# First layer of a two-layer decoder on one core: attention probabilities turned by VectorE and DRAM transfers in place of TensorE

## The chip, the core and the metric

The kernel runs on one core of one Trainium2 chip. The metric is the device time of one execution in microseconds (us). TensorE (PE, and PEld for its weight loads), VectorE (DVE), ScalarE (ACT) and GpSimd (POOL) each work through a list of instructions in order; SP issues the transfers of the weights, POOL the transfers told of below.

## The reference, cut to what matters

A trunk of two layers, 256 tokens of width 2048, all float32. The first layer is forgetting attention with 32 heads of 64, the second sliding-window attention; only the first is touched.

```python
p = rmsnorm(x, norm_g[0]) @ fox_w_in        # q, k, v, gate, forget logits
c = cumsum(log_sigmoid(forget logits + b_f))            # per head
s = einsum('qd,kd->qk', q, k) / 8 + c[q] - c[k]         # causal: k <= q
y = softmax(s) @ v * silu(gate)
x = x + y @ fox_w_out
```

Queries are swept in blocks of 128. For one head the first block sees 128 keys and the second 256, so the probabilities of a head are three blocks of 128 queries by 128 keys. The product with v contracts over keys, so keys must lie on the partitions: each block has to be turned.

## The kernel before

**Weights.** Every weight matrix comes in pieces of 512 KB (`wraw`, four buffers). ACT casts a piece to its high half (L222), DVE subtracts to get the low half (L223), both into `w` (five buffers), and TensorE multiplies high and low halves (`acc`). `mm` and `transpose` keep TensorE in the order in which the program is written.

**Groups.** The heads of layer one are eight groups of four, a group two pairs of heads (j = 0, 1). A group's units are q, k and gate, of 16 slices of the contraction each; an odd group also computes v for itself and the next one. When k of a group is there, `attend` hangs the attention steps on a clock: `tick()` counts, one step per two matmuls (in v units two steps per three), and `after(n, fn)` runs fn n steps later. So the tables `FOX_DUE`, `FOX_ODD`, `FOX_FIRST` and `FOX_NEXT` say between which weight matmuls each piece of attention stands.

**A pair.** `early` fetches the row -c[k] to all partitions (`bc`, a POOL transfer, L649) and masks it (L125, POOL), 14 steps ahead. `s` forms the scores of the second query block into the one score buffer in PSUM (`ps_s`), DVE adds the bias (L430) and finds the maxima (L411). `s_first` does the same for the first query block (L442) some steps later, in the same buffer. Then ACT takes exponentials (L359) and DVE normalises `st` (L367, L370). `t`, once per head, has TensorE turn three blocks by matmuls against the identity (`pt`, L84), and ACT copies them to `pts` (L451).

**Values.** At `due[2]`, an even group multiplies `pts` of the previous odd group and of its own with v (`psy`, 16 matmuls a group); groups 0 and 7 do so alone. DVE multiplies by the gate (L534), ACT and DVE split the result into `ys`. The tile `pts` of even groups and that of odd groups have one buffer each; `bc` and `st` have two.

**Layer two** already turns its probabilities by a DVE transpose of 32x32 blocks (L497), multiplies per 32-row strip, and sends v through DRAM once (`vs_d`, L889, L896, L897). That part stays.

Of the kernel before, what the change touches and what calls it, by code (L numbers as in the profile page):

```python
# [19 lines left out]
KT = D // P  # L20
H = 32
HD = 64
KVH = 4
ROT = 16
EPS = 1e-6
# [34 lines left out]
def trunk(  # L60
# [22 lines left out]
    def transpose(out, in_, ident):  # L83
        tc.keep_in_program_order(nc.tensor.transpose(out, in_, ident))  # L84
# [235 lines left out]
    def each(row):  # L320

        return row.unsqueeze(1).to_broadcast([P, 2, S])
# [69 lines left out]
    class Pair:  # L392
# [54 lines left out]
        def t(self, hh, group):  # L447
            pt = ps_t.tile([P, 512], F32, tag="T", name="pt")
            for b in range(3):
                transpose(pt[:, b * P : (b + 1) * P], self.st[:, hh, b * P : (b + 1) * P], ident)  # L450
            nc.scalar.copy(group.new_pts(self.j, hh)[:, hh, self.j, :], pt[:, 0 : 3 * P])  # L451

        def later(self, group, s, t, second=SECOND, bias=BIAS, other=4):
            self.second = second
            after(s - bias, self.early)
            after(s, self.s)
            after(t, lambda: self.t(0, group))
            after(t + other, lambda: self.t(1, group))

    class JointPair(Pair):  # L460

# [31 lines left out]
            after(t, lambda: self.both_t(group))  # L493

        def both_t(self, group):
            turned = group.new_pts(self.j, 0)[:, group.u % 2 * 2 + self.j]
            nc.vector.transpose(  # L497
                turned.rearrange("p h k -> p (h k)"), self.st.rearrange("p h k -> p (h k)")
            )

    class Group:
# [1 line left out]

        pts_home = work, "pts"

        def new_pts(self, j, hh):

            if j == hh == 0:
                pool, tag = self.pts_home
                self.pts = pool.tile([P, 2, 2, 3 * P], F32, tag=tag, name="pts", bufs=1)  # L510
            return self.pts

        def attend(self, kt, due, together, same):
            self.kt = kt
            for j, steps in enumerate(due[0:2]):
                self.pair(j).later(self, *steps)
            if together:
                after(due[2], lambda: self.values(together, same))

        def values(self, together, same):  # L520

            psys = []
            for G in together:
                psy = ps_t.tile([P, 512], F32, tag="T", name="psy")
                psys.append(psy)
                for js in [slice(0, 2)] if same else [slice(j, j + 1) for j in range(2)]:
                    for hh in range(2):
                        o = psy[hh * HD : (hh + 1) * HD, :].rearrange("p (j n) -> p j n", j=2)[:, js, :]
                        p = G.pts[:, hh, js, :]
                        v = [G.v_of(js.start, b, hh) for b in range(2)]  # L530
                        mm(o, v[0], p[:, :, 0:S], start=True, stop=False)
                        mm(o[:, :, P:S], v[1], p[:, :, S : 3 * P], start=False, stop=True)
# [51 lines left out]
    class FoxGroup(Group):  # L584
# [3 lines left out]
            self.g = g  # L588

        def q(self, ps):  # L590
            t = fox.tile([P, 2, S], F32, tag="q", name="q", bufs=1)
            nc.vector.tensor_add(t, ps[:, :, 0:S], low_half(ps))
            nc.vector.tensor_mul(t, t, each(state["r08"][:, 0:S]))
            self.qT = stack_q(t)

        def k(self, ps):
            t = fox.tile([P, 2, S], F32, tag="k", name="k", bufs=1)
            nc.vector.tensor_add(t, ps[:, :, 0:S], low_half(ps))
            nc.vector.tensor_mul(t, t, each(r0()[:, 0:S]))  # L599

            kk = self.kT = fox.tile([P, 2, 2, 2, S], F32R, tag="kk", name="kk", bufs=KBUFS)
            for hh, (w, other) in enumerate(((TOP, BOTTOM), (BOTTOM, TOP))):
                nc.scalar.copy(kk[w, :, hh, 0, :], t[w])
                nc.scalar.copy(kk[other, :, hh, 0, :], t[w])
                high = kk[w, :, hh, 0, :].bitcast(F32)
                nc.vector.tensor_sub(kk[w, :, hh, 1, :], t[w], high)  # L606
                nc.vector.tensor_sub(kk[other, :, hh, 1, :], t[w], high)  # L607
            due = (FOX_FIRST, FOX_NEXT, FOX_DUE, FOX_ODD)[min(self.g, 2 + self.g % 2)] if self.g < 7 else FOX_DUE
# [5 lines left out]
            self.attend(2 * self.g, due, mates, False)  # L614

        def v_pair(self, other):

# [278 lines left out]
                nc.gpsimd.dma_start(out=most[rows], in_=blocks[:, 0:6])  # L896
                nc.gpsimd.dma_start(out=rest[rows], in_=blocks[:, 6:8])  # L897

    B, NB = 32, P // 32
    vs_d = dram.tile([S, 256], F32, name="vs_d")  # L900

    class SwaGroup(Group):
# [5 lines left out]
        def q(self, ps):  # L908
            with tc.high_priority(HP):
                t, u = rotate(ps)  # L910
                nc.vector.tensor_add(t, t, u)
                self.qT = stack_q(t)

            self.attend(2 * self.u, SWA_DUE if self.u < 7 else SWA_LAST, (self.other, self) if self.u % 2 else (), True)

        def pair(self, j):
            h0 = 4 * self.u + 2 * j
# [18 lines left out]
            pair.bias = smask.unsqueeze(1).to_broadcast([P, 2, 3 * P])  # L936
            return pair

        def new_pts(self, j, hh):
# [5 lines left out]
        def values(self, together, same):  # L945

            if self.u < 7:
                self.some(together, range(NB), ps_s.tile([P, 2, 512], F32, tag="S", name="psy_s"))
                return
            self.some(together, range(2))  # L950
            after(LAST_HALF, lambda: self.some(together, range(2, NB)))

        def some(self, together, mine, pair=None):
# [25 lines left out]
            for g, G in enumerate(together):  # L979
# [224 lines left out]
```

## Time and profile before

| | |
|---|---|
| three timed runs | 813.56, 814.32, 814.44 us, median 814.32 |
| profiled execution, its own time | 814.33 us |
| its span, first to last instruction | 812.6 us |
| TensorE busy, granted clock | 802.0 us, 0.997 |
| DVE, ACT, POOL busy | 635.2, 529.6, 68.1 us |
| moved by transfers | 151.84 MB, mean 187 GB/s |

Work on layer one's attention lies between about 64 and 420 us of the span. Idle time of an engine costs only where TensorE, or whatever else sets the end, waits for it. A group's row in the list of groups gives how many instructions, their busy time in total and the mean of one; matmuls are pipelined, so their busy times overlap, and what a matmul takes from the end is better read from the chain of waits, whose pieces add up to the span.

### The profile page before, as it was taken

To read this page: it belongs to the slowest core of one execution; us is meant where nothing else is said; L and a number is where in the kernel's file an instruction comes from. 1 tells how busy PE (TensorE), PEld (TensorE's weight loads), DVE (VectorE), ACT (ScalarE), POOL (GpSimd) and SP (SyncE) were. 2 spreads that over 40 slices of the span, in tenths; PEclk is the share of its full clock that TensorE was granted. 3 is DMA by queue.
4 is the path that set the end of the run, shared out by engine and by line. 5 is a ranking of instruction groups with operands and counts; after the bars stand their busy time and mean duration, and the time that the engine had idled before them with its cause. 6 is when DMAs were issued, how large, how long until landed. Compare 5 with 4: busy or idle time off the path is not lost.

```text
span 812.6 us, 13809 instructions
## 1 busy us (share of the span) xinstructions
PE 802.0 (99%) x5090; PEld 705.6 (87%) x5090; DVE 635.2 (78%) x1132; ACT 529.6 (65%) x979; POOL 68.1 (8%) x102
## 2 busy tenths in 40 slices
PE   8999999999999999999999999999999999999996
PEld 7988788888888888888888888888888888888885
DVE  6988876887678776788847778678999999987654
ACT  6876665674756666575746555577788777875652
POOL 1012120010000100010003110200000000001210
PEclk9999999999999999999999999999999999999998
DMA  8767565564565655565455655766446544565632
GB/s 271 260 222 237 184 200 185 176 221 160 197 203 171 210 181 194 183 209 167 156 183 168 219 180 196 195 182 201 137 157 206 181 162 152 157 191 197 195 124 104
DMA packets 47730, 151.84 MB, mean 187 GB/s; under 512 B 5696, under 2 KB 7648, under 8 KB 47664
## 3 DMA queue, kind: packets, MB, share of 16 engines
q1 hardware_dynamic: 44640, 141.84, 53.6%
q0 software_dynamic: 1872, 7.67, 3.2%
q10 hardware_dynamic: 1152, 1.47, 0.5%
q8 instruction: 40, 0.66, 0.3%
q14 instruction: 26, 0.21, 0.1%
HBM read 148.55 MB, written 2.41 MB: 186 GB/s over the span
## 4 chain that ended last, share of the span: by engine, by line
PE 97%; DVE 2%; DMA 1%; ACT 0%; issue 0%; DVEq 0%; SPq 0%
PE acc L81 90%; PE ps_s L81 3%; PE psy L81 2%; PE pt L84 1%; DMA wraw<-in_vf_dram 1%; DVE w L223 0%; PE psy_s L81 0%; DVE st L370 0%; DVE scaled L836 0%; DVE q L389 0%; DVE kk L607 0%; ACT st L359 0%; DVE kk L606 0%; PE ps_n L81 0%; DVE k L599 0%
## 5 line engine op out<-in xcount | busy, mean ns | idle before, releaser
L81 PE MATMUL acc<-xs,w 128*128 128x256 f32 (+1 forms) x2624 | 473.1, 338 | 0.0
L81 PEld LDWEIGHTS acc<-xs,w 128*128 128x128 f32 x2624 | 405.7, 190 | 53.3 <-issue 0.7
L223 DVE TENSOR_TENSOR w<-wraw,w 128x1024 fp32r<-128x1024 f32 (+4 forms) x277 | 322.3, 1177 | 102.7 <-ACT w L222 101.8
L222 ACT CAST w<-wraw 128x1024 fp32r<-128x1024 f32 (+4 forms) x277 | 274.1, 1009 | 154.4 <-PE acc L81 122.2
L81 PE MATMUL acc<-ys,w 128*128 128x256 f32 (+1 forms) x960 | 168.8, 337 | 0.0
L81 PEld LDWEIGHTS acc<-ys,w 128*128 128x128 f32 x960 | 147.4, 190 | 19.3 <-issue 0.5
L81 PE MATMUL acc<-w,xs 128*128 128x512 f32 (+2 forms) x512 | 111.0, 364 | 1.5 <-ACT w L222 1.5
L81 PEld LDWEIGHTS acc<-w,xs 128*128 128x128 f32 x512 | 86.8, 190 | 15.8 <-ACT w L222 1.8
L359 ACT ACTIVATE st<-st,mx 128x256 f32<-128x256 f32 (+1 forms) x128 | 56.5, 443 | 12.5 <-DVE mx L411 7.1
L317 ACT COPY half<-acc 128x512 f32<-128x512 f32 x56 | 32.7, 584 | 36.9 <-PE acc L81 36.5
L741 POOL TENSOR_TENSOR acc<-acc,sq 128x256 f32<-128x256 f32 x28 | 26.7, 955 | 82.5 <-ACT sq L735 81.4
L81 PE MATMUL ps_s<-kk,q 128*128 128x256 f32 (+1 forms) x160 | 30.9, 306 | 0.2 <-DVE kk L607 0.2
L81 PEld LDWEIGHTS ps_s<-kk,q 128*128 128x128 f32 x160 | 24.7, 190 | 3.3 <-ACT pts L451 0.6
L649 POOL DMA_DIRECT2D bc<-negc_d x16 | 8.8, 553 | 220.4 <-DVE st L442 159.2
L125 POOL TENSOR_SCALAR_AFFINE_SELECT bc<-bc 128x256 f32<-128x256 f32 x32 | 21.7, 699 | 62.2 <-DMA bc<-negc_d 62.2
L739 POOL COPY acc<-sq 128x256 f32<-128x256 f32 x2 | 1.3, 636 | 288.2 <-ACT sq L735 288.2
L378 ACT ACTIVATE st<-st,rl 128x128 f32<-128x128 f32 x64 | 23.9, 445 | 0.4 <-ACT gate_e L335 0.3
L359 ACT ACTIVATION_READ_ACCUMULATOR st<-st,mx 128x1 f32 x128 | 24.0, 188 | 0.0
L157 DVE SCALAR_TENSOR_TENSOR xs<-xT,g_sb,xs 128x256 fp32r<-128x256 f32 x32 | 20.4, 666 | 3.5 <-ACT xs L156 3.5
L451 ACT COPY pts<-pt 128x384 f32<-128x384 f32 x32 | 15.2, 476 | 8.7 <-PE pt L84 8.5
L156 ACT ACTIVATE xs<-xT,g_sb 128x256 fp32r<-128x256 f32 x32 | 15.5, 502 | 8.1 <-DVE xT L721 7.4
L411 DVE CUSTOM_DVE_ANT_0 st<-ps_s,st 128x256 f32<-128x256 f32 (+1 forms) x64 | 20.2, 352 | 0.4
(144 smaller groups left out, 579.4 us busy)
## 6 DMA issues: line engine op xcount, KB each, us to landing
wraw<-in_fox_in_dram SPq DMA_DIRECT2D x96, 512.0 KB, 4.2
wraw<-in_swa_in_dram SPq DMA_DIRECT2D x72, 512.0 KB, 4.4
wraw<-in_fox_out_dram SPq DMA_DIRECT2D x32, 512.0 KB, 4.5
wraw<-in_swa_out_dram SPq DMA_DIRECT2D x32, 512.0 KB, 4.5
wraw<-in_fox_in_dram SPq DMA_DIRECT2D x54, 256.0 KB, 4.1
bc<-negc_d POOLq DMA_DIRECT2D x16, 384.0 KB, 4.6
wraw<-in_vf_dram SPq DMA_DIRECT2D x4, 288.0 KB, 5.8
xT<-in_xt_dram SPq DMA_DIRECT2D x2, 512.0 KB, 8.2
```

What stands on the lines that cost most here:

```text
L81: tc.keep_in_program_order(nc.tensor.matmul(*args, **kw))
L125: return nc.gpsimd.affine_select(out=ap, in_=ap, compare_op=ALU.is_ge, fill=NEG, base=base, pattern=pattern, channel_multiplier=mult,)
L156: nc.scalar.activation(xs[:, kt, 0, :], xT[:, kt, :], AF.Copy, scale=g)
L157: nc.vector.scalar_tensor_tensor(out=xs[:, kt, 1, :], in0=xT[:, kt, :], scalar=g, in1=xs[:, kt, 0, :].bitcast(F32), op0=ALU.mult, op1=ALU. ...
L222: state["split"] = nc.scalar.copy(high, raw)
L223: state["lows"] = [*state.get("lows", [])[-1:], nc.vector.tensor_tensor(out=low, in0=raw, in1=high.bitcast(F32), op=ALU.subtract)]
L317: nc.scalar.copy(s, ps[:, :, S : 2 * S])
L359: nc.scalar.activation(st[:, hh, rng], st[:, hh, rng], AF.Exp, scale=sign, bias=nm[:, qb, hh : hh + 1], accum_out=l[:, qb, hh : hh + 1],)
L378: nc.scalar.mul(st[:, hh, rng], st[:, hh, rng], rl[:, qb, hh : hh + 1])
L411: nc.vector.tensor_tensor_reduce(out=st, in0=high, in1=st if low is None else low, scale=self.scale, scalar=self.start(hh), op0=ALU.add, o ...
L451: nc.scalar.copy(group.new_pts(self.j, hh)[:, hh, self.j, :], pt[:, 0 : 3 * P])
L741: nc.gpsimd.tensor_add(sums[0], sums[0], s)
```

## The change

The method `t` goes, with its 96 turns on TensorE and 32 copies on ACT. A new method `turn` stands at the end of `s_first`, behind the normalisation. One DVE instruction transposes the pair's 128 x 768 probabilities in 32 x 32 blocks into `staged`, ordered by key block of 32; a POOL transfer writes that to DRAM (`turned_d`, 384 KB in rows of 768 bytes); four POOL transfers read it back, each into 32 partitions of `pts`, so that keys lie on partitions as before. The two halves of `psy` read `pts` through a view with runs of 32 queries. The tables change: the second score product is hung 12 to 16 steps behind the first, the values at 138, 122 (last group), 170 (first group), 120. The consumers of q and k get high priority in the ordering of ACT and DVE, and in layer two a rule that puts the gate products ahead of the weights' low halves now holds for the last group as well.

```diff
-FOX_DUE = ((21, 54, 12, 14, 2), (52, 86, 10, 14, 2), 112)
-FOX_ODD = ((21, 51, 12), (51, 82), 118)
-FOX_FIRST = ((57, 94, 15, 32), (80, 112), 127)
-FOX_NEXT = ((26, 57, 11), (57, 88), 118)
+FOX_DUE = ((21, 12), (52, 13), 138)
+FOX_LAST = ((24, 12), (48, 13), 122)
+FOX_ODD = ((22, 12), (51, 12), 118)
+FOX_FIRST = ((57, 16, 32), (81, 12), 170)
+FOX_NEXT = ((28, 12), (59, 14), 120)
...
             self.soft(self.st, self.mx)
-
-        def t(self, hh, group):
-            pt = ps_t.tile([P, 512], F32, tag="T", name="pt")
-            for b in range(3):
-                transpose(pt[:, b * P : (b + 1) * P], self.st[:, hh, b * P : (b + 1) * P], ident)
-            nc.scalar.copy(group.new_pts(self.j, hh)[:, hh, self.j, :], pt[:, 0 : 3 * P])
...
+            self.turn()
+
+        def turn(self):
+
+            staged = fox.tile([P, NB, 6, B], F32, tag="staged", name="staged", bufs=1)
+            nc.vector.transpose(
+                staged.rearrange("p b t i -> p t b i"),
+                self.st.rearrange("p h (t b i) -> p (h t) b i", b=NB, i=B),
+            )
+            turned_d = dram.tile([NB, P, 6 * B], F32, tag="turned_d", name="turned_d", bufs=2)
+            nc.gpsimd.dma_start(
+                out=turned_d.rearrange("b p x -> p b x"), in_=staged.rearrange("p b t i -> p b (t i)")
+            )
+            pts = self.group.new_pts(self.j)[:, self.j]
+            for b in range(NB):
+                nc.gpsimd.dma_start(
+                    out=pts[b * B : (b + 1) * B], in_=turned_d[b].rearrange("(a j) x -> j a x", j=B)
+                )
...
-                for js in [slice(0, 2)] if same else [slice(j, j + 1) for j in range(2)]:
+                for j in range(2):
                     for hh in range(2):
...
+                        o = psy[hh * HD : (hh + 1) * HD, j * S : (j + 1) * S]
+                        o = o.rearrange("p (q a i) -> p q a i", a=NB, i=B)
+                        p = G.pts[:, j].rearrange("p a (t i) -> p t a i", i=B)[:, 3 * hh : 3 * hh + 3]
+                        v = [G.v_of(j, b, hh) for b in range(2)]
+                        mm(o, v[0], p[:, 0:2], start=True, stop=False)
+                        mm(o[:, 1], v[1], p[:, 2], start=False, stop=True)
...
-            if pair is not None:
-                ahead_of_lows(last)
+            ahead_of_lows(last)
```

Three places show what the change does to the order of the engines; line numbers are those of each kernel, those of the changed one being 2 to 16 higher (its L83 is L81 here, L86 is L84, L225 is L223, L413 is L411, L444 is L442, L665 is L649, L127 is L125).

**TensorE, an even group (group 2), from the scores of the first query block of its second pair (`ps_s`, 256 wide) to its first product with v (`psy`).** Before:

```order
L81 MATMUL ps_s<-kk,q_1430 128x256 x2
L81 MATMUL acc<-xs,w 128x512 x20
L81 MATMUL acc<-xs,w 128x256 x28
L84 MATMUL pt<-ident,st 128x128 x3
L81 MATMUL acc<-xs,w 128x256 x4
L84 MATMUL pt<-ident,st 128x128 x3
L81 MATMUL acc<-xs,w 128x512 x16
L81 MATMUL acc<-w,xs 128x512 x24
L81 MATMUL psy<-pts,vg 64x256
```

The changed kernel:

```order
L83 MATMUL ps_s<-kk,q_1422 128x256 x2
L83 MATMUL acc<-xs,w 128x512 x14
L83 MATMUL acc<-xs,w 128x256 x32
L83 MATMUL acc<-xs,w 128x512 x16
L83 MATMUL acc<-w,xs 128x512 x33
L83 MATMUL ps_s<-kk,q_1774 128x512 x2
L83 MATMUL acc<-w,xs 128x512 x18
L83 MATMUL ps_s<-kk,q_1774 128x256 x2
L83 MATMUL acc<-w,xs 128x512 x12
L83 MATMUL psy<-pts,vg 64x256
```

The turns (`pt`) are gone, and the products with v stand later, behind both score products of the next group's first pair.

**POOL, about the first group.** `bc` is the bias of a pair; `turned_d` and `pts` are the new transfers; `sinks` belongs to layer two. Before:

```order
L649 DMA bc<-negc_d 128x768
L125 AFFINE_SELECT bc<-bc 128x2x128 x2
L649 DMA bc<-negc_d 128x768
L125 AFFINE_SELECT bc<-bc 128x2x128 x2
L655 DMA sinks<-in_sink_dram 128x32
```

The changed kernel, from the store of group 0's first pair to the loads of its second:

```order
L458 DMA turned_d<-staged 128x4x192
L665 DMA bc<-negc_d 128x768
L463 DMA pts<-turned_d 32x4x192 x4
L127 AFFINE_SELECT bc<-bc 128x2x128 x2
L665 DMA bc<-negc_d 128x768
L458 DMA turned_d<-staged 128x4x192
L127 AFFINE_SELECT bc<-bc 128x2x128 x2
L671 DMA sinks<-in_sink_dram 128x32
L463 DMA pts<-turned_d 32x4x192 x4
```

A store waits for DVE's transpose, and the four loads for the store to land; the bias of a later pair stands between them. From group 2 on each pair's rows are bias, mask, store, four loads.

**DVE, group 0's second pair and group 1's k (`kk`).** `L442`/`L444` is the bias added to the pair's first-block scores, `L367` to `L370` the normalisation. Before:

```order
L599 TENSOR_TENSOR k<-k,r_n_492 128x512
L367 RECIPROCAL rl<-l 128x4
L370 TENSOR_SCALAR st<-st,rl 128x128
L370 TENSOR_SCALAR st<-st,rl 128x256
L370 TENSOR_SCALAR st<-st,rl 128x128
L370 TENSOR_SCALAR st<-st,rl 128x256
L223 TENSOR_TENSOR w<-wraw,w 128x2x512
L606 TENSOR_TENSOR kk<-k,kk 64x2x256
L607 TENSOR_TENSOR kk<-k,kk 64x2x256
```

The changed kernel:

```order
L614 TENSOR_TENSOR k<-k,r_n_492 128x512
L444 TENSOR_TENSOR st<-ps_s,bc 128x2x128
L225 TENSOR_TENSOR w<-wraw,w 128x2x512
L621 TENSOR_TENSOR kk<-k,kk 64x2x256
L622 TENSOR_TENSOR kk<-k,kk 64x2x256
L621 TENSOR_TENSOR kk<-k,kk 64x2x256
L413 ISA st,mx<-ps_s,st 128x128
```

The work on k goes ahead: the pair's maxima (`L413`), and with them its normalisation and transpose, now come behind `kk`, where the normalisation stood ahead of it.

More of the change, by code (lines that the diff above doesn't have):

```diff
@@ L22 @@
 HD = 64
+B, NB = 32, P // 32
 KVH = 4
@@ L495, in both_t @@
         def both_t(self, group):
-            turned = group.new_pts(self.j, 0)[:, group.u % 2 * 2 + self.j]
+            turned = group.new_pts(self.j)[:, group.u % 2 * 2 + self.j]
             nc.vector.transpose(
@@ L517, in attend, with values @@
             if together:
-                after(due[2], lambda: self.values(together, same))
-        def values(self, together, same):
+                after(due[2], lambda: self.values(together))
+        def values(self, together):
             psys = []
@@ L590, in q @@
         def q(self, ps):
[L591 to L594, printed above, removed]
-        def k(self, ps):
[L597 to L608, printed above, removed]
+            with tc.high_priority(HP):
+                t = fox.tile([P, 2, S], F32, tag="q", name="q", bufs=1)
+                nc.vector.tensor_add(t, ps[:, :, 0:S], low_half(ps))
+                nc.vector.tensor_mul(t, t, each(state["r08"][:, 0:S]))
+                self.qT = stack_q(t)
+        def k(self, ps):
+            with tc.high_priority(HP):
+                t = fox.tile([P, 2, S], F32, tag="k", name="k", bufs=1)
+                nc.vector.tensor_add(t, ps[:, :, 0:S], low_half(ps))
+                nc.vector.tensor_mul(t, t, each(r0()[:, 0:S]))
+                kk = self.kT = fox.tile([P, 2, 2, 2, S], F32R, tag="kk", name="kk", bufs=KBUFS)
+                for hh, (w, other) in enumerate(((TOP, BOTTOM), (BOTTOM, TOP))):
+                    nc.scalar.copy(kk[w, :, hh, 0, :], t[w])
+                    nc.scalar.copy(kk[other, :, hh, 0, :], t[w])
+                    high = kk[w, :, hh, 0, :].bitcast(F32)
+                    nc.vector.tensor_sub(kk[w, :, hh, 1, :], t[w], high)
+                    nc.vector.tensor_sub(kk[other, :, hh, 1, :], t[w], high)
+            due = (FOX_FIRST, FOX_NEXT, FOX_DUE, FOX_ODD)[min(self.g, 2 + self.g % 2)] if self.g < 7 else FOX_LAST
             alone = self.g in (0, 7)
@@ L943, in new_pts, with values @@
             return self.other.pts
-        def values(self, together, same):
+        def values(self, together):
             if self.u < 7:
```

26 lines of the change are left out of this document (9 added, 17 removed).

## The prediction

> **What bounds the kernel now.** I read the page's shares first, then the chain that ended last, then what TensorE waited for.
>
> ```profile
> PE 802.0 (99%) x5090; PEld 705.6 (87%) x5090; DVE 635.2 (78%) x1132; ACT 529.6 (65%) x979; POOL 68.1 (8%) x102
> PE 97%; DVE 2%; DMA 1%; ACT 0%; issue 0%; DVEq 0%; SPq 0%
> PE acc L81 <- ACT w L222: 1.5, 1, 1.5
> PE ps_s L81 <- DVE kk L607: 0.2, 1, 0.2
> ```
>
> 97% of the chain is TensorE, and within layer one's attention its only wait is 0.2 us, for `kk` of group 1 (the 1.5 us lie at the start). So the end moves with what TensorE itself does there, as long as nothing new keeps it waiting. What a turn takes is read from the chain, whose pieces tile the time (start, length, what):
>
> ```profile
> 160.36 0.48 PE acc L81 x4
> 182.32 2.80 PE psy L81 x32
> 198.08 0.33 PE pt L84 x3
> 198.41 0.47 PE ps_s L81 x2
> 198.88 1.39 PE acc L81 x6
> 200.27 0.33 PE pt L84 x3
> 202.69 0.23 PE ps_s L81 x2
> ...
> 211.50 33.10 PE acc L81 x190
> ...
> 308.59 33.10 PE acc L81 x190
> ```
>
> Three turns of one head take 0.33 us; a 512-wide weight matmul 1.39/6 = 0.232 us, a 256-wide one 0.12.
>
> **What is removed.** 96 turns in 32 such threes: 32 x 0.33 = 10.6 us. 28 of them stand in the chain; the first four lie at 79 to 89 us, where the chain runs through DVE to `kk`. TensorE is busy there too, so their 1.3 us count if `kk` comes no later.
>
> ```profile
> 77.47 1.02 DVE L370 TENSOR_SCALAR st<-st,rl 128x128 f32<-128x128 f32 x4
> 89.03 0.69 DVE L607 TENSOR_TENSOR kk<-k,kk 64x512 fp32r<-64x512 f32 x1
> L389 DVE TENSOR_TENSOR q<-q,q 64x512 fp32r<-64x512 f32 x16 | 11.0, 686 | 0.5
> ```
>
> From the first pair's normalisation to the last part of `kk` DVE now takes 89.72 - 78.49 = 11.2 us. In the changed order there stand between: two splits (1.1 each), one transpose (1.0), ten instructions of 0.2 to 0.7 (halves of q, k's sum and scaling, the late bias, `kk`; most of them 64 to 128 x 512, 0.69 as in the last row): some 9.5 us, since the second pair's normalisation goes behind. I take the whole 10.6; without the four it is 9.2.
>
> ACT loses 32 copies, DVE gains 16 transposes.
>
> ```profile
> L223 DVE TENSOR_TENSOR w<-wraw,w 128x1024 fp32r<-128x1024 f32 (+4 forms) x277 | 322.3, 1177 | 102.7 <-ACT w L222 101.8
> L451 ACT COPY pts<-pt 128x384 f32<-128x384 f32 x32 | 15.2, 476 | 8.7 <-PE pt L84 8.5
> L497 DVE STREAM_TRANSPOSE turned<-st 128x768 f32<-128x768 f32 x16 | 15.6, 972 | 4.5 <-ACT st L378 4.3
> 75.00:417.00 342.00, 341.78 (x1964) 296.30 (x1963) 261.68 (x486) 217.74 (x377) 26.39 (x42) 1.00 0.58 188
> 504.00:730.00 226.00, 226.00 (x1665) 200.49 (x1667) 199.49 (x398) 171.01 (x377) 5.22 (x9) 1.00 0.56 175
> ```
>
> In the last two rows the third busy time is DVE's, the fourth ACT's. Layer two makes the same transpose of 128 x 768 in 0.97 us. ACT's 15.2 us are worth nothing to the end. DVE in layer one goes from 262 of 342 us (77%) to about 277 of 332 (84%); layer two runs at 199/226 = 88% with TensorE never idle, so the mean leaves room. What can cost is a place where the transpose stands ahead of something TensorE needs: the one score buffer.
>
> ```profile
> 158.94 0.63 PE L81 MATMUL ps_s<-kk,q 128*128 128x512 f32 x2
> 160.46 0.68 DVE L430 TENSOR_TENSOR st<-ps_s,bc 128x512 f32<-128x512 f32 x1
> 162.54 0.41 DVE L411 CUSTOM_DVE_ANT_0 st<-ps_s,st 128x256 f32<-128x256 f32 x1
> 163.78 0.40 PE L81 MATMUL ps_s<-kk,q 128*128 128x256 f32 x2
> 170.91 1.01 DVE L370 TENSOR_SCALAR st<-st,rl 128x128 f32<-128x128 f32 x4
> ```
>
> For a second pair DVE frees the buffer at 162.9 (last L411). In the changed order the first pair's second product comes two steps later (0.9 us), and its transpose (1.0) lies before L430: 164.8. TensorE's next product would start at 158.94 + 0.47 + 18 x 0.232 + 8 x 0.12 = 164.5, since the tables move it from 10 to 13 steps. That is a wait of 0.3 us in each of three even groups, and of about as much after group 1's first scores, where three splits now stand nearby. Bounds: nothing (the late pair has slack in ACT), and the full 0.97 at all 16 transposes, 15.5 us. I take 1.0 us, near the row worked out.
>
> **What is added on POOL.** Per pair a store and four loads. Their nearest rows are layer two's v, stored and read back once, and the bias:
>
> ```profile
> 516.75 0.75 POOL L889 DMA_DIRECT2D vs_d<-vs  x1 [22.22 <-DVE vs L580]
> 521.60 0.61 POOL L896 DMA_DIRECT2D vr<-vs_d  x1 [4.10 <-DMA vs_d<-vs]
> L896 POOL DMA_DIRECT2D vr<-vs_d x4: 577/578/607, 521.6 to 525.0; - x4
> DMA to landing us min/median/max: 7.5/7.8/8.6
> L649 POOL DMA_DIRECT2D bc<-negc_d x16: 536/553/577, 56.7 to 360.4; - x16
> DMA to landing us min/median/max: 4.0/4.6/7.1
> L125 POOL TENSOR_SCALAR_AFFINE_SELECT bc<-bc x32: 396/403/2565, 62.8 to 365.9; 128x256 f32<-128x256 f32 x32
> ```
>
> (The landing row under each transfer belongs to it.) The round trip, from the end of the transpose: store 0.75 + 4.1 until POOL goes on, three more issues 3 x 0.58 = 1.7 before the last load starts, landing 4.6 (one bias of 384 KB) to 7.8 (v, 1 MB in eight transfers): 11.2 to 14.4 us. If the mask of a bias stands in front and takes its long time (2 x 0.4 against up to 2.9 for two), up to 2 us more. I take 13.5, between the two since the four loads carry 384 KB in more pieces than the bias.
>
> Is that covered? Even group, second pair: by the order shown, from the start of its late product to `psy` stand 93 wide (21.6 us) and 32 narrow weight matmuls (3.8), two score products (0.70) and the late one itself (0.23): 26.3 us. The softmax takes 163.78 to 171.92, 8.1 us, the transpose 1.0; 17.2 us are left, and 2.1 more since this pair is read by the last 8 of 32 `psy` matmuls (24/32 x 2.80). 13.5 is covered by 5.8 us. The last group has 94 wide and 52 narrow: 28 us, more cover. Group 0 has least: its second pair's softmax goes behind `kk`, so its transpose ends not 9.1 but about 16.6 us after the late product (4.1 until its bias is added, then four splits, `kk`, group 1's first scores, normalisation, transpose: 12 to 12.5), and from 110 wide and 12 narrow matmuls and three more score products `psy` comes 28.4 us after it, this pair's part 0.75 later. 28.4 + 0.75 - 16.6 = 12.5 against 11.2 to 16.4: a wait of 0 to 3.9, once; I take 1.0. The mask and bias between store and loads are in that range; what waits behind them is the bias of group 2, whose scores come a whole group later.
>
> The Trainium skill ("DMA: Bandwidth & Descriptors", "Anatomy of one DMA — SWDGE (gpsimd) path") fits a GpSimd transfer as 2.0 us plus its bytes at 436 GB/s. That gives 2.6 us for the store of v, where this trace has 4.6 to landing: it disagrees, under load. By it the trip would be some 7 us, group 0 would not wait, and the sum would be 1.0 us lower.
>
> **Weights.** 16 x 768 KB = 12.6 MB more pass the 16 engines in 332 us. A piece of weights lands 4.2 us after issue in the median:
>
> ```profile
> wraw<-in_fox_in_dram SPq DMA_DIRECT2D x96, 512.0 KB, 4.2
> q0 software_dynamic: 380, 1.12, 16.0%
> ```
>
> The second row is POOL's queue from 500 to 530 us: 1.12 MB took 16% of 30 us, so 12.6 MB take 54 us of each engine, 16% of the stretch; the mean share goes from 0.58 to about 0.74. Four raw buffers, each spent in 2.8 us, ask for a piece 8.4 us ahead, so 4 us hide the delay; if that cover were gone, a store's 384 KB at 188 GB/s would hold weights for 2 us. I take nothing.
>
> **`psy`** keeps its 128 matmuls, 11.4 us in the chain; only the view changes. Runs of 32 are read in layer two:
>
> ```profile
> L81 PE MATMUL psy_s<-turned,vr 32*64 32x128 f32 x156 | 5.4, 273 | 0.0
> L84 PE MATMUL pt<-ident,st 128*128 128x128 f32 x96 | 15.7, 272 | 0.0
> ```
>
> A 128-wide matmul lasts 273 ns over runs of 32 and 272 without: nothing, against 11.4 if the rate halved. The gate rule of layer two's last group acts where TensorE does not wait; nothing.
>
> **The sum**, against the profiled execution's 814.33 us (1.7 around its span; the median of the runs shown is 814.32): 814.33 - 10.6 + 1.0 + 1.0 = 805.7 us.
>
> **Rivals.** (a) *DVE sets the pace:* the transpose lands in full on TensorE's wait for the score buffer at the eight second pairs, 8 x 0.97 = 7.8 us in place of 1.0: 812.5. For it: DVE's order above has 0.3 us too little; against: 88% in layer two costs nothing. (b) *The round trip is too long, and the kernel gets slower:* `psy` waits once it passes 12.5 us in group 0, 19.3 in three even groups, about 20 in the last. At 21 us the waits are 8.5 + 3 x 1.7 + 1.0 = 14.6: 814.33 - 10.6 + 1.0 + 14.6 = 819.3. It turns slower at about 20.3. For it: a mask lasted up to 2565 ns where 403 is usual, so POOL can be held up by 2.2 us; held so at all five issues the trip would be 13.5 + 10.8 = 24. Against: 16 bias issues took 536 to 577 ns, none held. The Trainium skill ("SBUF — State Buffer", "SBUF: two separate sides") says why it might: GpSimd cannot write a transfer's descriptors while DVE runs a mode that takes their shared port. No issue row here shows it. (c) *The strided view slows `psy`* by half its rate: 805.7 + 11.4 = 817.1; against it the two rows above. (d) *The change doesn't do what it says:* TensorE's turns vanish from its order but hid the supply of weights, so their time comes back as waits for `w` (ACT, DVE or late transfers) and only the new waits stay: 816.3. Against: TensorE waited once, 0.2 us, from 75 to 417 us.
>
> **How the numbers follow.** Forecast 0.72 (its own range 803.3, no new wait, to 808.6, group 0's 3.9 us); (a) 0.11; (b) 0.09; (c) 0.04; (d) 0.04. The range for 8 in 10, with (a) taken in by half, is 803.0 to 811.0. A measurement of this kernel tells about 0.2%, 1.6 us, from no change. Faster: 0.72 and most of (a), 0.81; within 0.2%: the edge of (a) and of (d), 0.06; slower: (b), (c), half of (d) and a little for what I have not seen, 0.13.
>
> **What would show it.** Right: no `pt` from layer one in the chain, `psy` still 2.80 us for 32, TensorE's waits for `pts` about 1 us in all and those for the score buffer under 2; DVE near 650 us busy, ACT near 514. Wrong in the first term: the span of two groups (211.5 to 308.6 before) shrinks by less than 2.0 us with no new wait named. Wrong on the trip: `psy` waiting on a transfer in groups 2, 4 and 6. The forecast falls if DVE's transposes last much over 1 us, or stores land after more than 8.

## The result, and the profile after

| | before | changed |
|---|---|---|
| median of the runs of one comparison | 813.89 us (12 runs, 812.98 to 818.26) | 808.70 us (12 runs, 805.63 to 812.98) |
| ratio, with its 95% interval | | 0.9938 (0.9916 to 0.9960) |
| profiled execution, its span | 814.33, 812.6 us | 806.58, 804.8 us |

The kernel gained 5.2 us at the median, and it lost its steadiness: eleven of the twelve runs of before lie within 1.5 us (the twelfth took 818.26), while the changed kernel's are spread over 7 us. The profiled execution is one of the quicker ones, 7.75 us ahead of the profile of before.

From the page of the changed kernel: busy times, the chain, and three rows of its list of transfers (median us to landing).

```profile
PE 791.6 (98%) x4994; PEld 695.0 (86%) x4994; DVE 646.9 (80%) x1148; ACT 516.5 (64%) x947; POOL 116.3 (14%) x182
PE 84%; DVE 7%; DMA 4%; ACT 2%; issue 2%; SPq 0%; POOL 0%; DVEq 0%; ACTq 0%
...
wraw<-in_fox_in_dram SPq DMA_DIRECT2D x96, 512.0 KB, 4.9
...
turned_d<-staged POOLq DMA_DIRECT2D x16, 384.0 KB, 4.8
pts<-turned_d POOLq DMA_DIRECT2D x64, 96.0 KB, 5.3
```

TensorE is busy 10.4 us less (802.0 before). But the chain, 97% TensorE before, is now 84%: DVE, transfers and ACT hold 13%. In three stretches (244 to 275, 339 to 371 and 384 to 413 us of the span) it leaves TensorE for the engines behind a wait of 0.5, 0.9 and 1.0 us. So 13% is not the time that is lost; it marks where the other engines have no slack left. TensorE's waits, and the same stretch that the prediction used (third busy time DVE, fourth ACT, then the share of the transfer engines before the last column):

```profile
PE ps_s L83 <- DVE kk L622: 1.4, 2, 0.9
PE acc L83 <- ACT w L224: 1.4, 3, 0.9
PE psy L83 <- DMA pts<-turned_d: 1.0, 1, 1.0
PE ps_s L83 <- DVE mx L413: 0.5, 1, 0.5
...
75.00:417.00 342.00, 339.06 (x1911) 293.15 (x1910) 276.86 (x505) 207.45 (x348) 74.13 (x122) 1.00 0.74 229
```

The 1.4 us for `w` lie at the start, as the 1.5 us did before. TensorE's idle time in the stretch went from 0.2 us (342.00 - 341.78) to 2.9. The named parts of it are 0.5 for the score buffer (group 1), 1.4 for `kk` (groups 5 and 7) and 1.0 for the last group's `pts`. With the turns they make the profiled result: -10.6 + 0.5 + 1.4 + 1.0 = -7.7, against -7.75. The transfers' share is 0.74, as estimated.

### The profile page after: what moved, and what is told of

Its sections match the earlier page's. It is cut to its first block, busy times and chain, and to the rows that moved or that the text cites. A ratio compares the mean times of both kernels' runs of the same rounds, so it can differ in the third digit from the quotient of the medians.

```text
span 804.8 us, 13739 instructions
## 1 busy us (share of the span) xinstructions
PE 791.6 (98%) x4994; PEld 695.0 (86%) x4994; DVE 646.9 (80%) x1148; ACT 516.5 (64%) x947; POOL 116.3 (14%) x182
## 4 chain that ended last, share of the span: by engine, by line
PE 84%; DVE 7%; DMA 4%; ACT 2%; issue 2%; SPq 0%; POOL 0%; DVEq 0%; ACTq 0%
PE acc L83 79%; DMA wraw<-in_fox_in_dram 3%; PE ps_s L83 2%; PE psy L83 2%; DVE w L225 2%; DMA pts<-turned_d 1%; ACT st L361 1%; DMA turned_d<-staged 1%; DVE st L372 1%; DVE staged L453 1%; DVE st L413 1%; DVE kk L622 1%; DVE kk L621 1%; PE psy_s L83 0%; ACT w L224 0%
## 5 line engine op out<-in xcount | busy, mean ns | idle before, releaser
L83 PE MATMUL acc<-xs,w 128*128 128x256 f32 (+1 forms) x2624 | 468.2, 337 | 0.3 <-ACT w L224 0.3
L83 PEld LDWEIGHTS acc<-xs,w 128*128 128x128 f32 x2624 | 404.6, 190 | 53.7 <-issue 0.7
L225 DVE TENSOR_TENSOR w<-wraw,w 128x1024 fp32r<-128x1024 f32 (+4 forms) x277 | 322.7, 1179 | 87.6 <-ACT w L224 86.6
L83 PE MATMUL acc<-ys,w 128*128 128x256 f32 (+1 forms) x960 | 168.3, 337 | 0.0
L83 PEld LDWEIGHTS acc<-ys,w 128*128 128x128 f32 x960 | 147.7, 190 | 19.4 <-issue 0.5
L83 PE MATMUL acc<-w,xs 128*128 128x512 f32 (+2 forms) x512 | 108.3, 361 | 1.1 <-ACT w L224 1.1
L83 PEld LDWEIGHTS acc<-w,xs 128*128 128x128 f32 x512 | 86.9, 188 | 16.1 <-ACT w L224 1.6
L463 POOL DMA_DIRECT2D pts<-turned_d x64 | 35.2, 556 | 55.5 <-DMA turned_d<-staged 40.2
L83 PE MATMUL ps_s<-kk,q 128*128 128x256 f32 (+1 forms) x160 | 31.1, 307 | 2.0 <-DVE kk L622 1.4
L127 POOL TENSOR_SCALAR_AFFINE_SELECT bc<-bc 128x256 f32<-128x256 f32 x32 | 22.5, 720 | 70.4 <-DMA bc<-negc_d 70.4
L83 PEld LDWEIGHTS ps_s<-kk,q 128*128 128x128 f32 x160 | 24.8, 190 | 6.1 <-issue 3.0
L665 POOL DMA_DIRECT2D bc<-negc_d x16 | 9.0, 560 | 115.2 <-issue 101.6
L413 DVE CUSTOM_DVE_ANT_0 st<-ps_s,st 128x256 f32<-128x256 f32 (+1 forms) x64 | 20.3, 350 | 0.5
```

The lines of the kernel that those rows point to most:

```text
L83: tc.keep_in_program_order(nc.tensor.matmul(*args, **kw))
L127: return nc.gpsimd.affine_select(out=ap, in_=ap, compare_op=ALU.is_ge, fill=NEG, base=base, pattern=pattern, channel_multiplier=mult,)
L225: state["lows"] = [*state.get("lows", [])[-1:], nc.vector.tensor_tensor(out=low, in0=raw, in1=high.bitcast(F32), op=ALU.subtract)]
L413: nc.vector.tensor_tensor_reduce(out=st, in0=high, in1=st if low is None else low, scale=self.scale, scalar=self.start(hh), op0=ALU.add, o ...
L463: nc.gpsimd.dma_start(out=pts[b * B : (b + 1) * B], in_=turned_d[b].rearrange("(a j) x -> j a x", j=B))
```

## Where the last group waits

The last group in the changed kernel: TensorE's rows from its late product to `psy`, then DVE's transpose, POOL's store and four loads, and the last load's piece of the chain (start, length).

```profile
388.34 0.40 PE L83 MATMUL ps_s<-kk,q 128*128 128x256 f32 x2
...
389.96 20.94 PE L83 MATMUL acc<-ys,w 128*128 128x512 f32 x116
410.83 0.88 PE L83 MATMUL psy<-pts,vg 128*64 128x256 f32 x8
412.68 0.88 PE L83 MATMUL psy<-pts,vg 128*64 128x256 f32 x8 [0.97 <-DMA pts<-turned_d]
...
397.32 0.97 DVE L453 STREAM_TRANSPOSE staged<-st 128x768 f32<-128x768 f32 x1
...
398.59 0.76 POOL L458 DMA_DIRECT2D turned_d<-staged  x1 [6.34 <-DVE staged L453]
404.61 2.19 POOL L463 DMA_DIRECT2D pts<-turned_d  x4 [5.26 <-DMA turned_d<-staged]
...
406.25 6.30 DMA pts<-turned_d
```

From the late product to the second pair's part of `psy` TensorE has 410.83 + 0.88 - 388.34 = 23.4 us of work. Softmax and transpose take 9.95 of it (to 398.29), the trip 14.26 (the last load lands at 412.55): 24.2. So it comes 0.8 us late by this sum, and TensorE stands 0.97.

## Experiments

Each was compared with the kernel before on the same chip. "Before" and "changed" name the two kernels of this document.

**1. Without transfers.** The transpose writes straight to the layout of `pts`; store and loads go. The sorting into partitions is left out, so the values are multiplied with unsorted blocks.

```diff
-            staged = fox.tile([P, NB, 6, B], F32, tag="staged", name="staged", bufs=1)
+            pts = self.group.new_pts(self.j)[:, self.j]
             nc.vector.transpose(
-                staged.rearrange("p b t i -> p t b i"),
+                pts.rearrange("p b (t i) -> p t b i", i=B),
...
-            (store to turned_d and the four loads)
```

> The changed kernel without its transfers: VectorE's block transpose writes straight into the tile that TensorE reads, so probabilities are not sorted into their partitions (that part of the computation is left out); TensorE, VectorE and ScalarE have the same instructions. If transfers cost the changed kernel its missing microseconds and its spread, whether by delaying weights (A) or by being waited for (B): 803.5 to 804.5 us, all runs within 1.5 us, TensorE's waits in layer one under 1 us. If it is the order on VectorE and the one score buffer (C): no better than 806, the waits for the score buffer and for k stay.

**2. Transfers that nobody reads.** As 1, but the store is made from `pts` and the four loads fill a tile that is not used. The sorting is left out here too.

```diff
+            nc.gpsimd.dma_start(out=turned_d.rearrange("b p x -> p b x"), in_=pts)
+            unread = fox.tile([P, NB, 6 * B], F32, tag="staged", name="unread", bufs=1)
...
-                    out=pts[b * B : (b + 1) * B], in_=turned_d[b].rearrange("(a j) x -> j a x", j=B)
+                    out=unread[b * B : (b + 1) * B], in_=turned_d[b].rearrange("(a j) x -> j a x", j=B)
```

> The changed kernel with all its transfers, of the same size and at the same place, but into a tile that nobody reads; TensorE reads what VectorE's block transpose wrote (so the sorting is left out of the result). A (they delay the weights): as the changed kernel, median 807 to 809.5, spread 5 us or more, weights landing up to 8 us, TensorE waiting for k and w. B (the products with v wait for them): as without transfers, 803.5 to 804.5.

**3. The changed kernel once more**, no edit.

> The changed kernel once more, unaltered, for a second execution's trace and more times: 805.5 to 813, median near 808.7. Where it is longer than the 804.8 us span of the first trace, the extra waits of TensorE are for k and weights (A) or for the turned probabilities (B).

**4. The kernel before with the transfers.** Its turns on TensorE stay; the untransposed probabilities are stored and loaded into an unused tile.

```diff
             self.soft(self.st, self.mx)
+            self.turn()
+            (turn: one store of self.st to turned_d, four loads into "unread")
```

> The kernel before, with TensorE's turns, plus the 16 stores and 64 loads of the changed kernel, from the untransposed probabilities into a tile that nobody reads. A: 1 to 6 us above the kernel before, spread over 3 us. B: as the kernel before, within 1 us, since nothing waits for them.

| | median, range (runs) | before | ratio, 95% |
|---|---|---|---|
| 1 no transfers | 803.59, 802.48 to 804.92 (4) | 814.43 | 0.9868 (0.9851 to 0.9884) |
| 2 unread | 807.37, 806.36 to 809.18 (4) | 814.43 | 0.9918 (0.9902 to 0.9935) |
| 3 changed again | 809.69, 804.86 to 811.74 (6) | 814.43 | 0.9935 (0.9905 to 0.9964) |
| 4 before + transfers | 814.04, 813.40 to 814.63 (10) | 814.43 | 0.9996 (0.9986 to 1.0005) |

What follows: the change without its transfers gains 10.8 us (1), about the 10.6 of the turns. The transfers cost 3.8 us even when nobody reads them (2 against 1); in the profile of 2 TensorE waits 2.8 us for `kk` in groups 3, 5 and 7, in that of 1 not at all:

```profile
PE ps_s L83 <- DVE kk L620: 2.8, 4, 0.9
```

That they are also read adds about 2 us at the median (the changed kernel and 3 against 2, each by its ratio), but the intervals overlap, so this is not shown. Yet in the old order the transfers cost nothing (4): my expectation that they would slow any kernel fell. It takes the transfers together with the rest of the change, which I call the new order: its tables and priorities, the transposes on DVE, no turns. The trace shows a link in ACT's waits for late weights, from 110 to 417 us (us in total, times, longest); rows of the changed kernel, then of 2, 4 and 1:

```profile
ACT w L224 <- DMA wraw<-in_fox_in_dram: 5.9, 8, 1.6
ACT w L224 <- DMA wraw<-in_fox_out_dram: 2.5, 2, 1.7
```

```profile
ACT w L224 <- DMA wraw<-in_fox_in_dram: 8.3, 6, 2.5
ACT w L224 <- DMA wraw<-in_fox_out_dram: 2.2, 2, 1.7
```

```profile
ACT w L223 <- DMA wraw<-in_fox_in_dram: 0.2, 1, 0.2
```

```profile
ACT w L224 <- DMA wraw<-in_fox_in_dram: 0.2, 1, 0.2
```

Pieces of weights land after 4.6 us (4) or 4.8 (2), almost the same; but only the new order has ACT standing there when they are late. Why the old order is not caught out, no run settles; the rows behind experiment 8 show where it had room.

In the profile of experiment 3 the last group waited 3.0 us for its transfer, and then something else cost more. TensorE's waits, and its stretches (length, busy time, granted clock, share and rate of the transfers):

```profile
PE psy L83 <- DMA pts<-turned_d: 3.0, 1, 3.0
...
416.00:418.00 2.00, 1.82 (x13) 0.76 0.03 10
418.00:420.00 2.00, 2.00 (x11) 0.50 0.49 131
420.00:422.00 2.00, 2.00 (x13) 0.89 0.19 45
```

Behind the wait the granted clock fell to 0.50: 2 x (0.24 + 0.50 + 0.11) = 1.7 us are lost again. In the first profile, after a wait of 1.0, it stayed at 1.00. The longer wait (2.1 us more), the clock (1.7) and one more wait of 0.9 at group 5's scores make 4.7 of the 5.0 us by which this span (809.8) exceeds the first profile's (804.8): here the read transfer (B) is the larger part.

**5. The scores of groups 3 and 5 later.** A theory K: the wait for `kk` is there because the values no longer stand between k's unit and the first score product.

```diff
-FOX_ODD = ((22, 12), (51, 12), 118)
+FOX_ODD = ((28, 12), (54, 12), 118)
```

> The changed kernel with the scores of groups 3 and 5 put 6 steps later (first pair 28 in place of 22, second 54 in place of 51): 9 more wide products, 9 x 0.23 = 2.1 us more between k's unit and the first score product. Theory K (late weights delay the splits, the splits delay kk on VectorE, and the first score product waits because the values no longer stand ahead of it): the waits for kk in groups 3 and 5 vanish, in group 7 they stay; time 806.0 to 807.5, against 808.7 of the changed kernel. Rival C (the transfers slow the whole stretch through the weights, the place of the wait is chance): 808 to 809.5, with waits of about the same sum under another name (acc for w). The last group's wait for its transfer stays under both, and so does the spread of several us between runs.

**6. The last group's values later.**

```diff
-FOX_LAST = ((24, 12), (48, 13), 122)
+FOX_LAST = ((24, 12), (48, 13), 137)
```

> The changed kernel with the values of the last group put at 137 in place of 122 steps: 20 narrow and 10 wide products, 20 x 0.114 + 10 x 0.23 = 4.6 us more cover for its round trip. Theory L (the last group's trip is longer than its cover): the wait of psy for the transfer, 1.2 and 4.8 us in the two profiles of the changed kernel, vanishes or stays under 0.5; time 806.0 to 807.5; the slowest runs (811 to 813) disappear. Rival: what follows the values (gate and split, then the last part of the output weights) is late in its place, and PE waits for ys instead: 808 to 810.

**7. Both.**

```diff
-FOX_LAST = ((24, 12), (48, 13), 122)
-FOX_ODD = ((22, 12), (51, 12), 118)
+FOX_LAST = ((28, 12), (48, 13), 137)
+FOX_ODD = ((28, 12), (54, 12), 118)
```

> Both together, and the first pair of the last group 4 steps later too (28 in place of 24). Theories K and L: what remains is the changed kernel without its transfers (803.6) and little more: 803.6 to 805.5, with a spread of under 3 us between runs, no wait for kk over 0.3 us and none for pts. Rival C: 806 to 808, the waits have moved on to the supply of weights (acc for w, and ACT for wraw).

**8. Kernel 4 with the values where the change puts them.** Group 7 keeps 112.

```diff
-FOX_DUE = ((21, 54, 12, 14, 2), (52, 86, 10, 14, 2), 112)
+FOX_DUE = ((21, 54, 12, 14, 2), (52, 86, 10, 14, 2), 138)
```

> The kernel before with the unread transfers (814.0, wait for kk 0.2), and the values of groups 1 to 6 put at 138 steps in place of 112, so that they no longer stand between k's unit and the first score product of groups 3, 5 and 7: 2.8 us less cover at each. Theory K: waits for kk of 0.5 to 1 us in two or three of these groups, time 815 to 817. Rival (the cover was lost by the turns' removal or by the new order on VectorE and not by the place of the values): 814.0, wait for kk still 0.2.

| | median, range (runs) | before | ratio, 95% |
|---|---|---|---|
| 5 scores later | 808.86, 803.82 to 810.96 (6) | 814.22 | 0.9924 (0.9899 to 0.9949) |
| 6 last values later | 810.08, 806.57 to 811.29 (6) | 814.22 | 0.9956 (0.9943 to 0.9969) |
| 7 both | 807.06, 806.71 to 808.32 (4) | 814.22 | 0.9918 (0.9906 to 0.9931) |
| 8 old, values later | 813.96, 813.46 to 818.00 (12) | 814.22 | 1.0006 (0.9995 to 1.0017) |

None came out as expected in full. 5 has no wait for `kk` left, in group 7 neither, and its two best runs are at 804; its other four are at 808 to 811, and only the best one was profiled. The medians of 5 and 7 lie where rival C had put them, but neither profile shows the waits for `w` that C asked for. 6 lost the wait for the transfer (in the rows 1.0 and 3.0 us, the latter with 1.7 of clock, where its expectation speaks of 1.2 and 4.8) but, as its rival said, TensorE waits for `ys` in its place; its wait for `kk` stays, 0.9 us. 7 has the same wait for `ys` and no other new one (row of 7):

```profile
PE acc L83 <- DVE ys L554: 2.4, 1, 2.4
```

And 7 is steadier: 1.6 us between its four runs where the six of 5 and of 6 have 7 and 5. That fits two waits which both feed the scatter. It is not shown: the runs are few, and whether the slower runs of 5 waited for `pts`, no profile says.

8 refutes K in its first form: in the old order the values may stand late, with 0.3 us of wait for `kk` and no change of the median (two of its twelve runs took 817 and 818 us, as one of before did). What does make `kk` late is seen by laying group 3 of both kernels side by side. Changed kernel, profile of experiment 3: TensorE's first matmul after k's unit and the halted score product; DVE's normalisation and transpose of the pair before, then k's sum and the last part of `kk`:

```profile
173.00 7.64 PE L83 MATMUL acc<-w,xs 128*128 128x512 f32 x33
180.48 0.39 PE L83 MATMUL ps_s<-kk,q 128*128 128x512 f32 x1
181.67 0.47 PE L83 MATMUL ps_s<-kk,q 128*128 128x512 f32 x1 [0.80 <-DVE kk L622]
...
172.69 1.01 DVE L372 TENSOR_SCALAR st<-st,rl 128x128 f32<-128x128 f32 x4
...
174.75 0.97 DVE L453 STREAM_TRANSPOSE staged<-st 128x768 f32<-128x768 f32 x1
175.65 0.65 DVE L613 TENSOR_TENSOR k<-acc,half 128x512 f32<-128x512 f32 x1
...
180.83 0.69 DVE L622 TENSOR_TENSOR kk<-k,kk 64x512 fp32r<-64x512 f32 x1
```

Kernel 8, the same rows:

```profile
176.54 7.42 PE L82 MATMUL acc<-w,xs 128*128 128x512 f32 x32
183.79 0.61 PE L82 MATMUL ps_s<-kk,q 128*128 128x512 f32 x2
...
170.73 1.01 DVE L371 TENSOR_SCALAR st<-st,rl 128x128 f32<-128x128 f32 x4
...
177.35 0.69 DVE L612 TENSOR_TENSOR k<-acc,half 128x512 f32<-128x512 f32 x1
...
181.94 0.69 DVE L621 TENSOR_TENSOR kk<-k,kk 64x512 fp32r<-64x512 f32 x1
```

The cover is the same, 33 or 32 wide products. In 8 k's sum starts 0.8 us after the unit, and `kk` is whole at +6.1, with 1.2 us to spare. In the changed kernel the normalisation of group 2's second pair comes just then, a split and the new transpose behind it, and k's sum starts at +2.65: `kk` is whole at +8.5, where the product stands at +7.5. Without transfers (1) it starts at +1.6 and is whole at +7.4, with nothing to spare. The same rows of 1:

```profile
173.13 7.64 PE L83 MATMUL acc<-w,xs 128*128 128x512 f32 x33
180.61 0.63 PE L83 MATMUL ps_s<-kk,q 128*128 128x512 f32 x2
...
171.61 1.01 DVE L372 TENSOR_SCALAR st<-st,rl 128x128 f32<-128x128 f32 x4
...
174.69 0.65 DVE L604 TENSOR_TENSOR k<-acc,half 128x512 f32<-128x512 f32 x1
...
179.87 0.69 DVE L613 TENSOR_TENSOR kk<-k,kk 64x512 fp32r<-64x512 f32 x1
```

DVE's order is the same in 1 and in experiment 3; what moved it is seen on ACT. Two rows of experiment 3, a cast and the first exponential of that pair, then the first exponential in 1:

```profile
169.63 1.05 ACT L224 CAST w<-wraw 128x1024 fp32r<-128x1024 f32 x1 [1.92 <-DMA wraw<-in_fox_in_dram]
170.58 0.40 ACT L361 ACTIVATE st<-st,mx 128x128 f32<-128x128 f32 x1
...
169.50 0.40 ACT L361 ACTIVATE st<-st,mx 128x128 f32<-128x128 f32 x1 [0.64 <-DVE mx L669]
```

The exponentials stand behind a cast whose weights came late, and start 2.4 us ahead of the unit's end in place of 3.6. These 1.2 us go on to the normalisation (0.3 ahead in place of 1.5) and to `kk` (+8.5 in place of +7.4). The room itself went with the new order: from the late product to the end of the transpose group 2's second pair takes 12.55 us in 1 (162.21 to 174.76), where in 8 its normalisation ends 8.1 us after that product (163.60 to 171.74). This is read from the rows of one group; which part of the new order took the room was not run by itself. That with some 2 us more cover TensorE no longer waits for `kk` is what 5 and 7 show.

**9. The last group by TensorE**, the rest as changed.

```diff
         def turn(self):
+            if self.group.g == 7:
+                for hh in range(2):
+                    after((24, 34)[self.j] + 2 * hh, lambda hh=hh: self.t(hh))
+                return
...
+        def t(self, hh):          # three turns into "pt", one ACT copy to the blocks of pts
```

> The changed kernel with one thing undone: the last group's probabilities are turned by TensorE again (12 turns, 12 x 0.11 = 1.3 us) and go through no transfer; all else as changed. Theory L (the last group's round trip is longer than its 22 us of cover, by 1.2 and 4.8 us in two profiles, and is most of the spread between runs): 808.7 + 1.3 - 1.2 to 4.8, so 805.5 to 808, without runs above 810; the waits for kk in groups 3, 5 and 7 stay, 1 to 3 us in all. Rival (the spread comes from the transfers of all groups, wherever their readers are): 808 to 810 with a spread of 5 us or more.

**10. The same, with the scores later** (FOX_ODD as in 5, FOX_LAST's first pair at 28).

> The last group turned by TensorE, and the scores of groups 3 and 5 six steps later, of group 7 four. Theories K and L together: the changed kernel without any transfer (803.6) and 12 turns (1.3): 804.0 to 806.0, spread under 2.5 us, no wait for kk over 0.3 us, none for pts. Rival C (waits move on to the supply of weights): 806.5 to 808.5, acc waiting for w 2 us or more.

**11. As 7, the last values at 130.**

```diff
-FOX_LAST = ((28, 12), (48, 13), 137)
+FOX_LAST = ((28, 12), (48, 13), 130)
```

> As with both put later (807.1, of which 2.4 us PE waits for ys), but the last group's values at 130 steps in place of 137, 1.8 us of weight products after their first place. The wait for ys falls to under 0.5; the last group's trip is then uncovered by 0 to 3 us in some runs: 804.5 to 806.5, spread 2 to 4 us. If the trip in this order is as short as in its profile (loads landed ahead of 414.4), no psy wait and 804.7.

**12. As 9, without the priority of q and k.**

```diff
-            with tc.high_priority(HP):
-                t = fox.tile([P, 2, S], F32, tag="k", name="k", bufs=1)
+            t = fox.tile([P, 2, S], F32, tag="k", name="k", bufs=1)
...
```

> The kernel with the last group by TensorE, and the high priority taken off q and k of layer one (the other part of the change undone): k's sum, its product with the norm and the splits kk then stand behind more splits of weights on VectorE and ScalarE. Theory K: the waits for kk at the first score products grow by 1 to 2 us each in groups 1, 3, 5 and 7: 2 to 6 us slower than with the last group by TensorE alone. Rival (the priority changes the order but nothing waits for it): the same within 1 us.

| | median, range (runs) | before | ratio, 95% |
|---|---|---|---|
| 9 last by TensorE | 809.28, 807.28 to 813.81 (12) | 813.99 | 0.9949 (0.9933 to 0.9966) |
| 10 and scores later | 806.91, 805.86 to 808.61 (5) | 813.99 | 0.9916 (0.9904 to 0.9928) |
| 11 both later, 130 | 804.76, 803.58 to 806.00 (4) | 813.99 | 0.9888 (0.9875 to 0.9900) |
| 12 no priority | 810.56, 809.48 to 813.18 (6) | 813.99 | 0.9963 (0.9949 to 0.9976) |

9 refutes L as the one source of the scatter: without any trip in the last group the runs still lie 6.5 us apart, and its profile waits for `kk` three times and once, for 0.4 us, for group 0's `pts`; row of `kk`:

```profile
PE ps_s L83 <- DVE kk L635: 1.8, 3, 1.0
```

10 has the `kk` waits gone and the scatter down to 2.8 (five runs). It stays 0.9 us above the range expected, where rival C had put it, but without C's waits for `w`: in its profile group 6's values wait, in the part that the second pair fills. TensorE's row, then that pair's transpose and POOL's rows:

```profile
382.73 0.88 PE L83 MATMUL psy<-pts,vg 128*64 128x256 f32 x8 [1.20 <-DMA pts<-turned_d]
...
364.69 0.97 DVE L457 STREAM_TRANSPOSE staged<-st 128x768 f32<-128x768 f32 x1
...
365.89 1.78 POOL L127 TENSOR_SCALAR_AFFINE_SELECT bc<-bc 128x256 f32<-128x256 f32 x2 [7.85 <-DMA bc<-negc_d]
367.62 0.78 POOL L462 DMA_DIRECT2D turned_d<-staged  x1
373.09 2.20 POOL L467 DMA_DIRECT2D pts<-turned_d  x4 [4.68 <-DMA turned_d<-staged]
```

POOL works in order. The mask of a later pair's bias stands ahead of the store; it waited until its bias had landed and then took 1.78 us, where two masks mostly take 0.8. So the store, whose data were ready at 365.66, was issued 2.0 us later, and a load then took 7.9 us to land (374.19 to 382.11 in the chain; the median is 5.7). In such a run the trip is too long in an even group as well. Group 2's values stand 0.9 us at the same place, with no releaser that the profile names.

11 came out as expected and is the best kernel of the study: 9.2 us ahead of before, where the kernel without transfers is 10.8 ahead, and steady, with 2.4 us between its four runs. Its profile has no wait for `kk`, `pts` or `ys`, though ACT still waits 11.0 us for late weights: they reach TensorE no more, since what they delay now has cover. From 70 to 420 us TensorE waits only 0.6 us, for the score buffer.

12 is slower than 9 by 1.3 us at the median, with intervals that overlap: not told apart in time. In its profile TensorE waits four times for `kk`, where 9 has three waits of at most 1.0 us; the longest, 2.0 us, is in group 1, and the clock falls behind it:

```profile
PE ps_s L83 <- DVE kk L633: 4.2, 4, 2.0
```

## Why the prediction was right, and where it was not

The forecast of 805.7 us lies 3.0 us under the median of 808.7, inside the range of 803.0 to 811.0, and on the right side. That the range held is in part luck: its upper end stood there for rival (a), a wait for the score buffer, and what filled it were waits that the sum had put at nothing. Point by point:

- **The turns, -10.6: right.** Without transfers the kernel gains 10.8 us (experiment 1). The estimate that `kk` of group 1 would come no later also held: from the normalisation (78.51) to the last part of `kk` (87.75) it took 9.2 us, forecast 9.5, before 11.2.
- **The score buffer, +1.0: half of it.** The wait came once, after group 1's first scores as the text said, and lasted 0.5 us; the even groups did not wait.
- **Group 0, +1.0 (0 to 3.9): none in the changed kernel's profile,** 0.4 in experiment 9.
- **The trip, 13.5 us: right in size, short in the slower case.** 14.3 in the last group of the first profile, 16.3 in experiment 3 (399.72 to 416.04), with no mask in between; landings of store and load 4.8 and 5.3 in the median of the changed kernel.
- **"The softmax takes ... 8.1 us, the transpose 1.0": too short.** Both were read from the old order. From the late product to the end of the transpose it took 12.55, 13.3 and 13.5 us in groups 2, 4 and 6 of the first profile, and 12.55 in group 2 without transfers. So 3.4 to 4.4 of the 5.8 us of cover were not there, and group 6 could wait in experiment 10; the same delay stands ahead of k's sum.
- **"The last group has 94 wide and 52 narrow: 28 us, more cover": wrong.** By its rows 116 weight products stand behind the six wide ones: 70 wide and 52 narrow, 70 x 0.232 + 52 x 0.12 = 22.5 us. I had counted 24 wide products too many, 5.6 us, so the group named as the safest was the one with a wait: 1.0 us in one profile, 3.0 and 1.7 of lost clock in the other.
- **"4 us hide the delay", "I take nothing" for the weights: the main error.** ACT waited 8.4 us for late weights where it had waited 0; unread transfers alone cost 3.8 us. They reach TensorE through the order of ACT and DVE: late weights hold the pair's exponentials, so its normalisation and transpose push k's sum back, and `kk` of an odd group, which I did not cost beyond group 1, ends after its 7.5 us of cover. The test set for the first term shows it: between the starts of `psy` of groups 2, 4 and 6 lie 95.05 and 96.66 us, 97.08 and 97.19 before. They shrank by 2.0 and 0.5, with a wait for `kk` in each (0.5 and 0.9); without transfers they shrank by 2.7 and 1.7.
- **Rivals.** (b) in its full size did not come. Its mask is seen in experiment 10, where it held one store for 2.0 us; issues were not held (16 stores took 761 to 797 ns, 64 loads 551 to 675). (c) is refuted: 32 `psy` matmuls hold 2.80 us of the chain, as before. (d) did not come: without transfers the turns' whole time was won. (a) names the engine that is late at `kk`, though at another place, and at 1.4 us instead of 7.8.
- **DVE 650 and ACT 514:** 646.9 and 516.5.
- **Two figures do not follow from their own terms:** with no new wait the sum is 803.7, not 803.3, and in (b) the kernel turns slower at a trip of 20.0 us, not 20.3. Neither enters the forecast.

## What to carry to other kernels

When a change takes work from the engine that sets the pace, count anew the cover of everything that this work hid: here the engine got 10.6 us faster, and chains on other engines that had ended a microsecond early now end late. Read such a chain in the new order: here softmax and transpose took 3.4 us more than the old order's rows said. Give transfers on a shared queue, and what stands behind the weights, more cover than the median needs; here some 2 us each. Both covers together won 4.0 us at the median (experiment 11 against the changed kernel, each in its own comparison), either alone nothing that the runs tell apart. A spread between runs that a change brings is itself a hint: some wait may have lost its slack.

## What the runs showed of the chip that I had not expected

A wait of TensorE can cost more than it lasts. In three profiles it was followed by a stretch of half clock that lost 1.70 us each time: behind 3.0 us (experiment 3), 2.4 (experiment 7, rows below) and 2.0 with 0.8 shortly ahead (experiment 12, at clocks of 0.88, 0.50 and 0.77 for 2 us each). But the same wait for `ys`, 2.4 us, lowered nothing in experiment 6, nor did 1.0 in the changed kernel.

```profile
418.00:420.00 2.00, 1.61 (x6) 0.85 0.95 362
420.00:422.00 2.00, 2.00 (x7) 0.50 0.08 33
422.00:424.00 2.00, 2.00 (x11) 0.80 0.00 0
```

The Trainium skill ("TensorE: Matmul & The Clock Gate", "What's actually happening") says that the clock is halved by an activity monitor with a window of 3.4 us that runs freely and does not start anew with the kernel. The traces agree: the loss is 1.7 us, half of 3.4, and equal waits differ in whether it comes. They differ from the page in that it speaks of an idle window, and waits of 2.0 to 3.0 us were enough. So the same wait of 2.4 us cost 2.4 in experiment 6 and 4.1 in experiment 7; that its place in the window decides is not shown. The clock is part of the scatter: of the changed kernel's twelve runs the three with a mean clock of 0.993 to 0.995 took 810.8 to 813.0 us, the nine at 0.996 to 0.998 took 805.6 to 811.6. The rest of the scatter stays open, since two runs of the changed kernel and one of each other were profiled.
